# Dilated mixer of a hybrid decoder layer: a written order with weight halves split two steps ahead, softmax sums transposed before they go to DRAM, and first scores at the end of the gate projection

## The chip, the core and the metric

The kernel runs on one core of one Trainium2 chip. The metric is the device time of one execution in microseconds (us). Before the change the runs have a median of 2697.38 us over three runs (2695.77 to 2700.28). The engines are named as in the profile: PE multiplies (PEld are its weight loads), ACT is the scalar engine, DVE the vector engine, POOL the gpsimd engine, and SP only issues DMAs. DMAs are also issued by ACT and POOL, each in the order of its own instructions.

## What is computed

One decoder layer over 512 tokens of width 2048, in float32: a modulated RMSNorm gives `u`; one wide projection of `u` feeds three token mixers (differential attention, retention, dilated windows); each mixer's output is multiplied by a SiLU gate, projected, weighted by a sigmoid gate and summed; an output projection, a residual and a last norm follow. The change touches the dilated mixer only:

```
for each of 8 heads, three groups (window, dilation) = (128,1), (512,4), (2048,16), head dim 128:
    s_g   = q_g @ k_g^T / sqrt(128), masked to t, t-d, ..., t-window
    o_g   = softmax(s_g) @ v_g ;  den_g = log sum exp(s_g)
    o     = sum_g softmax over g (den_g) * o_g
y_C = o * silu(z_C)            # z_C: gate columns of the projection of u
```

With 512 tokens the second and third group are both sets of tokens that are equal modulo 4 (the third additionally masked), so both are computed on the same strided view, and their exponentials and sums are taken over one row of 2 x 128 scores against a common lowest score. The first group (a band of 128 tokens) is computed apart, with its own lowest score and its own sum; the two are merged by weights for which the first group's lowest scores and sums are needed in the strided token order.

## The kernel before

**Arithmetic.** Every float32 operand is split into a high part (ACT copies it to the multiply type) and a low part (DVE subtracts that copy from the original). A product is three matmuls, high x high, high x low and low x high (`mm3`, L164 to L166).

**Stages.** Before the mixer a long stage of block products writes most projections of `u` to DRAM: the queries of all groups, the keys of the first and second (`qk_dram`) and the values (`v_dram`). Only the third group's keys and the gate `z` are projected in the mixer itself. The mixer stands between 1372.71 and 1671.23 us of the profiled execution; the gate phase of its output projection follows.

**The mixer before (L844 to L1048).** A loop over 8 heads; each head does:

- The projection of the third group's keys: two weight halves of 1024 x 128 (512 KB), each loaded by SP (L136, tile `wr`), split by ACT (L159, `wh`) and DVE (L160, `wl`), then multiplied (24 matmuls of 128x512). Between the halves, the head before is turned (`turn`: 8 transposes of its exponentials, L931, split by L205/L206 into `p1`, `p2`), and the second group's scores are taken (`scores(1)`, L897/L899).
- After both halves: the values' products of the head before (`values`, L944/L946, and `mm3` for the first group), `first_turn` (7 transposes, L882, split by L885/L886 into `p0`), and the split of the projected keys out of PSUM (`split_pairs`, tile `kc<-pj`, L205/L206).
- The values of the head are loaded (L1000) and split (L1002/L1003), and the first group's query and key of the next head are loaded straight into `ql` and `kc` (`first_inputs`, L977/L978) and split (L979 and L982 on ACT, L980 and L983 on DVE). `qh`, `ql` and `kc` have two buffers each.
- The projection of `z`, again two halves. Between them: the third group's scores (`scores(2)`, L897/L899 with the projected keys), the masked negated scores with row minima on DVE (L903, L839), the exponentials on ACT (L913), the merge weights (`wt`), and then the first scores and first exponentials of the next head (`first_scores`: `mm3`, L839, L865).
- SiLU (sigmoid on ACT L211, product on DVE L213), and the next head's second query and key (`turned`, L988, L197/L198, L205/L206).

Two round trips through DRAM turn columns into rows. The first group's row minima and sums (`st1`, 128 partitions x 2 x 4 values) are written by a DMA that ACT issues (L869, `bounce<-st`, element by element with a stride of 512 bytes in partition order) and read back by a DMA that POOL issues (L870, `st<-bounce`) in strided token order. The merge weights `wt` are written likewise (L922) and read back broadcast to all partitions (L924, `wtb<-bounce`), where POOL multiplies them into the SiLU gate (`weigh`, L962) and DVE into the first group's output (L957).

**What sets the order.** The stage before the mixer is pinned: `pin` marks its matmuls, splits and loads to stay in the order of the program. The mixer is not: there, the scheduler of the tile layer puts each engine's instructions in an order of its own choice, and each engine then works through its list strictly in that order, waiting at an instruction whose inputs or buffers are not ready.

Of the kernel before, what the change touches and what calls it, by code (L numbers as in the profile page):

```python
# [2 lines left out]

# [61 lines left out]
def hybrid_kernel(ctx, tc, x, c, w_in, w_pa, w_pb, w_pc, w_out, w_ada, b_ada, norm_w, lam,  # L65
# [3 lines left out]
    act = nc.scalar  # L69
    dve = nc.vector  # L70
# [34 lines left out]
    nc.sync.dma_start(out=ident, in_=k_ident)  # L105
# [28 lines left out]
    def w_load(src, k0, c0):  # L134
        r, h, l = w_tiles([P, 8, P])
        nc.sync.dma_start(out=r, in_=src[k0:k0 + 1024, c0:c0 + P].rearrange("(j p) c -> p j c", p=P))  # L136
        return r, h, l

    pinned = [False]

    def pin(instr):

        if pinned[0]:
            tc.keep_in_program_order(instr)

    def w_half(src, k0, c0, rot=False, tiles=None, low=dve):
# [11 lines left out]
        else:  # L158
            pin(act.copy(h, r))  # L159
            pin(low.tensor_sub(l, r, h.bitcast(F32)))  # L160
        return h, l

    def mm3(ps, ah, al, bh, bl, start, stop):
        pin(nc.tensor.matmul(ps, lhsT=ah, rhs=bh, start=start, stop=False))  # L164
        pin(nc.tensor.matmul(ps, lhsT=ah, rhs=bl, start=False, stop=False))  # L165
        pin(nc.tensor.matmul(ps, lhsT=al, rhs=bh, start=False, stop=stop))  # L166
# [16 lines left out]
    def split(pool, tag, ps, shape=None, scale=None, view=None, bufs=1):  # L183

        shape = shape or [P, S]
        h = pool.tile(shape, F32R, tag=tag + "h", name=tag + "h", bufs=bufs)
        l = pool.tile(shape, F32R, tag=tag + "l", name=tag + "l", bufs=bufs)
# [14 lines left out]
    def split_pairs(pool, tag, src, bufs=1):  # L202

        t = pool.tile([P, 4, 2, P], F32R, tag=tag, name=tag, bufs=bufs)
        act.copy(t[:, :, 0, :], src)  # L205
        dve.tensor_sub(t[:, :, 1, :], src, t[:, :, 0, :].bitcast(F32))  # L206
        return t
# [8 lines left out]
    def v_load(pool, unit, c0, tag, strided=False):  # L216
# [4 lines left out]
        nc.sync.dma_start(out=r, in_=src.rearrange("(i r) c -> i r c", r=4) if strided  # L221
# [17 lines left out]
    nc.sync.dma_start(out=smalls[0:16, :], in_=c.rearrange("o (j p) -> (o j) p", p=P))  # L239
    nc.sync.dma_start(out=smalls[16:32, :], in_=norm_w.rearrange("o (j p) -> (o j) p", p=P))  # L240
    nc.sync.dma_start(out=smalls[32:80, :], in_=b_ada.rearrange("o (j p) -> (o j) p", p=P))
    nc.sync.dma_start(out=smalls[80:81, :], in_=da_w)
    nc.sync.dma_start(out=smalls[81:82, :], in_=ret_w)
    xt = [xq.tile([P, D], F32, tag=f"x{i}", name=f"x{i}") for i in range(NT)]
    for i in range(2):
        nc.sync.dma_start(out=xt[i], in_=x[0, i * P:(i + 1) * P, :])
# [8 lines left out]
    def mod_load():  # L255
# [10 lines left out]
        nc.sync.dma_start(out=wa, in_=w_ada[0, part * nk * P:(part + 1) * nk * P, half * D + c0:half * D + c0 + cw]  # L266
# [7 lines left out]
    def load_first(i):  # L274
# [3 lines left out]
        nc.sync.dma_start(out=r, in_=w_in[k * P:(k + 1) * P, g0:g0 + NF * P].rearrange("p (b c) -> p b c", c=P))  # L278
# [9 lines left out]
    nc.sync.dma_start(out=xt[2], in_=x[0, 2 * P:3 * P, :])  # L288
    for q in range(2):
        nc.sync.dma_start(out=xt[3][:, q * 1024:(q + 1) * 1024], in_=x[0, 3 * P:4 * P, q * 1024:(q + 1) * 1024])  # L290
# [10 lines left out]
    nc.tensor.transpose(tp[:, 0:P], smalls, ident)  # L301
# [25 lines left out]
    def mod_cols(m):  # L327
# [5 lines left out]
        for ci in range(nch):  # L333
            for a in range(chains):
                nc.tensor.matmul(pc[:, ci:ci + 1], lhsT=acc[:, a, ci * P:(ci + 1) * P], rhs=ones[:, 0:1],
# [31 lines left out]
    def x_tr(tp, i, k):  # L367
        nc.tensor.transpose(tp[:, i * P:(i + 1) * P], xt[i][:, k * P:(k + 1) * P], ident)
# [54 lines left out]
    for i, (phase, k) in enumerate(steps):  # L423
# [21 lines left out]
        for b in range(NF):  # L445
            nc.tensor.matmul(ps[b], lhsT=h[:, b, :], rhs=uh[k], start=k == 0, stop=False)
        if i + 1 < 2 * KC and i + 1 != KC and (i + 1) in group_of:
            mod_cols(group_of[i + 1])
        for b in range(NF):
            nc.tensor.matmul(ps[b], lhsT=h[:, b, :], rhs=ul[k], start=False, stop=False)  # L450
        for b in range(NF):
            nc.tensor.matmul(ps[b], lhsT=l[:, b, :], rhs=uh[k], start=False, stop=k == KC - 1)
# [28 lines left out]
    nc.sync.dma_start(out=lamt, in_=lam.rearrange("o a b -> (o a b)").partition_broadcast(P))  # L481
# [924 lines left out]
```

## Time and profile before

| | |
|---|---|
| runs, median (lowest to highest) | 2697.38 us (2695.77 to 2700.28) |
| the profiled execution's own time | 2697.8 us |
| its span, first to last instruction | 2696.0 us |
| PE busy, share of the span | 2563.4 us, 95% |
| DVE busy | 1912.5 us, 71% |
| ACT busy | 1130.1 us, 42% |
| mixer, 1372.71 to 1671.23 | 298.52 us: PE 259.64, DVE 180.41, ACT 159.30, POOL 21.62 busy |
| mean granted TensorE clock, whole span / mixer | 0.979 / 0.92 |

How to read the profile: times are microseconds from the span's start. A group of instructions is one line of the kernel, one engine and one operation, `out<-in` by tile names. In brackets stands the time that the engine stood idle just before an instruction, and the instruction or DMA that ended that wait. PE's busy time includes matmuls that run at a lower granted clock.

### The profile page before, as it was taken

Reading aid. Unit: us, or ns where it says so; the run is one execution under the profiler, and the core shown is the slowest. Engines: PE = TensorE matmul, PEld = TensorE weight load, DVE = VectorE, ACT = ScalarE, POOL = GpSimd, SP = SyncE. Lnnn points to the kernel's source line nnn. Section 1 sums busy time; section 2 is a strip of 40 time slices with the busy share of each in tenths; the row PEclk is TensorE's granted clock in tenths of the full one; section 3 lists DMA queues with packets and bytes.
Section 4 is the critical chain, followed back from the end, with each engine's and each line's share of the span. In section 5 each row is a group of like instructions: output and inputs, shape, how many; then the busy total and the mean of one; then the engine's idle time right before and its main releaser. Section 6 shows DMA issues by size and latency. Waiting matters only on the chain.

```text
span 2696.0 us, 36917 instructions
## 1 busy us (share of the span) xinstructions
PE 2563.4 (95%) x14531; PEld 2246.5 (83%) x14531; DVE 1912.5 (71%) x2646; ACT 1130.1 (42%) x1453; POOL 293.5 (11%) x336
## 2 busy tenths in 40 slices
PE   6999999999999999999998898999999989999898
PEld 5777778999999999998877777888888778878678
DVE  7995878777788777888766565357677457676674
ACT  4233433433334333333345555246666235553222
POOL 2331002221122212121000000000000000000000
PEclk9999999999999999999998999999999989999999
DMA  9776666666666666666665555552323563336862
GB/s 346 246 277 234 220 206 232 233 223 207 208 218 229 225 222 221 200 225 227 229 169 129 122 116 135 178 153 81 95 84 88 171 198 99 101 97 199 298 224 103
DMA packets 394418, 503.33 MB, mean 187 GB/s; under 512 B 27170, under 2 KB 258420, under 8 KB 393092
## 3 DMA queue, kind: packets, MB, share of 16 engines
q1 hardware_dynamic: 364484, 448.89, 52.9%
q0 software_dynamic: 10048, 35.23, 4.1%
q10 hardware_dynamic: 19712, 16.85, 1.8%
q8 instruction: 114, 1.87, 0.3%
q14 instruction: 60, 0.49, 0.1%
HBM read 449.39 MB, written 51.51 MB: 186 GB/s over the span
## 4 chain that ended last, share of the span: by engine, by line
PE 67%; DVE 13%; DMA 13%; ACT 4%; issue 3%; SPq 0%; ACTq 0%; DVEq 0%
PE at L166 11%; PE at L165 11%; PE at L164 11%; PE pj L164 10%; PE pj L165 10%; PE pj L166 10%; DVE acc L324 4%; DMA gpr<-part 2%; DMA ql<-qk 2%; DVE xl L513 2%; DMA gwa<-in_w_ada_dram 2%; DMA xr<-in_w_in_dram 1%; DMA gsg<-g 1%; DVE xr L598 1%; DVE wl L160 1%
## 5 line engine op out<-in xcount | busy, mean ns | idle before, releaser
L512 ACT CAST xh<-xr 128x2048 fp32r<-128x2048 f32 x196 | 374.3, 1910 | 586.9 <-PE at L165 349.1
L513 DVE TENSOR_TENSOR xl<-xr,xh 128x2048 fp32r<-128x2048 f32 x196 | 452.0, 2306 | 194.1 <-ACT xh L512 192.5
L166 PE MATMUL pj<-uh,wl 128*128 128x512 f32 x912 | 360.1, 395 | 5.7 <-DVE wl L157 3.1
L164 PE MATMUL pj<-uh,wh 128*128 128x512 f32 x912 | 363.6, 399 | 0.8 <-ACT wh L156 0.8
L165 PE MATMUL pj<-ul,wh 128*128 128x512 f32 x912 | 359.5, 394 | 0.0
L598 DVE TENSOR_TENSOR xr<-xr 128x512 f32<-128x512 f32 x448 | 329.8, 736 | 18.5 <-DMA xr<-in_w_in_dram 7.0
L160 DVE TENSOR_TENSOR wl<-wr,wh 128x1024 fp32r<-128x1024 f32 x146 | 178.1, 1225 | 121.1 <-ACT wh L159 116.7
L166 PE MATMUL at<-fh,xl 128*128 128x256 f32 x864 | 246.0, 285 | 4.3 <-DVE xl L513 4.3
L164 PE MATMUL at<-fh,xh 128*128 128x256 f32 x864 | 245.2, 284 | 0.0
L165 PE MATMUL at<-fl,xh 128*128 128x256 f32 x864 | 245.2, 284 | 0.0
L159 ACT CAST wh<-wr 128x1024 fp32r<-128x1024 f32 x148 | 154.5, 1050 | 204.3 <-PE pj L165 84.4
L166 PEld LDWEIGHTS pj<-uh,wl 128*128 128x128 f32 x912 | 173.6, 190 | 43.0 <-DVE wl L157 3.5
L164 PEld LDWEIGHTS pj<-uh,wh 128*128 128x128 f32 x912 | 174.6, 191 | 35.5 <-ACT wh L156 1.3
L165 PEld LDWEIGHTS pj<-ul,wh 128*128 128x128 f32 x912 | 174.1, 191 | 34.5
L166 PEld LDWEIGHTS at<-fh,xl 128*128 128x128 f32 x864 | 166.2, 192 | 5.6 <-DVE xl L513 5.5
L165 PEld LDWEIGHTS at<-fl,xh 128*128 128x128 f32 x864 | 166.3, 192 | 0.0
L164 PEld LDWEIGHTS at<-fh,xh 128*128 128x128 f32 x864 | 166.2, 192 | 0.0
L165 PE MATMUL at<-ul,xh 128*128 128x256 f32 x576 | 163.0, 283 | 0.0
L164 PE MATMUL at<-uh,xh 128*128 128x256 f32 x576 | 163.0, 283 | 0.0
L166 PE MATMUL at<-uh,xl 128*128 128x256 f32 x576 | 163.0, 283 | 0.0
L164 PE MATMUL at<-yh,wh 128*128 128x512 f32 x336 | 132.7, 395 | 6.4 <-DVE gsg L809 6.4
L165 PE MATMUL at<-yl,wh 128*128 128x512 f32 x336 | 131.8, 392 | 0.0
(421 smaller groups left out, 5954.0 us busy)
## 6 DMA issues: line engine op xcount, KB each, us to landing
xr<-in_w_in_dram SPq DMA_DIRECT2D x224, 512.0 KB, 4.5
xr<-in_w_in_dram SPq DMA_DIRECT2D x84, 1024.0 KB, 5.1
wr<-in_w_in_dram SPq DMA_DIRECT2D x116, 512.0 KB, 3.9
wa<-in_w_ada_dram SPq DMA_DIRECT2D x20, 1024.0 KB, 9.7
wr<-in_w_out_dram SPq DMA_DIRECT2D x32, 512.0 KB, 4.7
gwa<-in_w_ada_dram SPq DMA_DIRECT2D x32, 512.0 KB, 4.9
wr<-in_w_in_dram SPq DMA_DIRECT2D x32, 448.0 KB, 7.1
wb<-in_w_ada_dram SPq DMA_DIRECT2D x12, 1024.0 KB, 10.6
```

What stands on the lines that cost most here:

```text
L159: pin(act.copy(h, r))
L160: pin(low.tensor_sub(l, r, h.bitcast(F32)))
L164: pin(nc.tensor.matmul(ps, lhsT=ah, rhs=bh, start=start, stop=False))
L165: pin(nc.tensor.matmul(ps, lhsT=ah, rhs=bl, start=False, stop=False))
L166: pin(nc.tensor.matmul(ps, lhsT=al, rhs=bh, start=False, stop=stop))
L324: dve.scalar_tensor_tensor(out=acc, in0=wa[:, j, :], scalar=sc[:, k:k + 1], in1=acc, op0=ALU.mult, op1=ALU.add)
L512: pin(act.copy(h, r))
L513: pin(dve.tensor_sub(l, r, h.bitcast(F32)))
L598: pin(dve.tensor_add(r[:, o, :], r[:, o, :], r[:, a, :]))
```

## The change

- **Pinning.** All instructions of ACT, DVE, PE and SP now go through a wrapper that marks them to keep program order while `pinned[0]` is set. Where the stage before the mixer pinned its instructions one by one, the wrapper does the same. `pinned[0]` is now also set for the whole mixer. (In the changed kernel, instructions issued through the wrapper carry its line, L86.)
- **A written pipeline.** The mixer's 32 weight halves are steps: of head `hd`, steps `4 * hd` and `4 * hd + 1` are the two halves of the third keys' projection (k0, k1 from here on), `4 * hd + 2` and `4 * hd + 3` those of the gate `z` (z0, z1). `half_step(n)` issues in this order: the load of half n+4, extra loads of the mixer, the split of half n+2, the work that was put off until here (`late`), and the 24 matmuls of half n. Scores, turns and values stand between the steps.
- **First scores** of the next head move from the middle of the z projection to its end.
- **First sums.** `st1` is turned on PE (one transpose to 8 x 128), copied by ACT to a row tile and written by one DMA with 8 rows of 512 bytes. It is issued after the second half of the k projection, and POOL reads it back as before.
- **Small things.** The raw third and second queries and the second keys have a tile each (`r2`, `r3`, `r4`) instead of two shared buffers `rq`; `lows` has one buffer instead of two; the mask `tri` is a part of the `band` tile, and its DMA is dropped; values, first queries and keys are loaded and split in separate functions so that each can be placed.

The core of the diff:

```diff
+    class Ordered:
+        def __init__(self, engine):
+            self.engine = engine
+        def __getattr__(self, name):
+            f = getattr(self.engine, name)
+            return lambda *a, **k: pin(f(*a, **k))
+
+    act, dve, pe, sync = (Ordered(e) for e in (nc.scalar, nc.vector, nc.tensor, nc.sync))
...
-            bounce = dram.tile([2, S], F32, tag="bounce", name="bounce", bufs=2)
-            nc.scalar.dma_start(out=bounce.rearrange("s (a p) -> p s a", p=P), in_=st1)
-            nc.gpsimd.dma_start(out=st[:, 2:4, :], in_=bounce.rearrange("s (i r) -> i s r", r=4))
+        def first_sums():
+            tp = at()
+            pe.transpose(tp[0:8, 0:P], ctx_["st1"].rearrange("p s a -> p (s a)"), ident)
+            row = cp.tile([8, P], F32, tag="row", name="row")
+            act.copy(row, tp[0:8, 0:P])
+            bounce = dram.tile([8, P], F32, tag="bounce", name="bounce", bufs=2)
+            act.dma_start(out=bounce, in_=row)
+            nc.gpsimd.dma_start(out=ctx_["st"][:, 2:4, :], in_=bounce.rearrange("(s a) (i r) -> (a i) s r", s=2, r=4))
...
+    def half_step(n, *extra):
+        half_load(n + 4)
+        for f in extra:
+            f()
+        if loads:
+            entry.append(w_half(w_in, 0, 0, tiles=loads.pop(0)))
+        due, late[:] = list(late), []
+        for f in due:
+            f()
+        half_mul(n)
...
+    for hd in range(8):
+        h, prev = heads[hd], heads[hd - 1] if hd else None
+        def more():
+            got["raw3"] = load_turned(4, hd)
+            if hd < 7:
+                got["raw2"] = load_turned(2, hd + 1), load_turned(3, hd + 1)
+        half_step(4 * hd, more)
+        if prev:
+            prev.turn()
+            prev.weigh(sz)
+        else:
+            h.first_scores(*first[0], first[1])
+            late.append(h.first_exps)
+        h.scores(1, *second[0], second[1])
+        def more():
+            third[:] = query_tiles(), key_tiles()
+            if hd < 7:
+                got["first"] = load_first_qk(hd + 1)
+        late.append(lambda: split_query(got["raw3"], third[0]))
+        half_step(4 * hd + 1, more)
+        split_keys(half_ps[0], third[1])
+        if prev:
+            h.first_sums()
+            prev.values(vs)
+            h.first_turn()
+            late.append(lambda: prev.finish(sz))
+        if hd < 7:
+            late.append(lambda: split_first_qk(*got["first"]))
+        half_step(4 * hd + 2, lambda: got.update(vs=load_values(hd)))
...
+        h.scores(2, *third[0], third[1])
+        late.append(h.exps)
+        if hd < 7:
+            late.append(lambda: got.update(
+                second=(split_query(got["raw2"][0], query_tiles()), split_keys(got["raw2"][1], key_tiles()))))
+        half_step(4 * hd + 3)
+        sz = silu(cp, half_ps[0], bufs=1)
+        vs = got["vs"]
+        if hd < 7:
+            heads[hd + 1].first_scores(*got["first"][0], got["first"][1])
+            late.append(heads[hd + 1].first_exps)
+            second = got["second"]
+        late.append(lambda vs=vs: split_values(vs))
```

How instructions move is shown at three places. The first is ACT in a middle head, around the split of the projected third keys (`kc<-pj`); the numbers are those of tile buffers. Before:

```order
L205 CAST p1_13052<-at_13047 128x4x128
L205 CAST p2_13060<-at_13055 128x4x128
L979 ACTIVATE qh_13193<-ql_13194 128x512
L159 CAST wh_13342<-wr_13341 128x1024
L205 CAST kc_13175<-pj_13016 128x4x128
L950 COPY gpr_13113<-at_13114 128x2x128
L950 COPY gpr_13113<-at_13125 128x2x128
L982 CAST kc_13195<-kc_13195 128x4x128
L885 CAST p0h_13154<-at_13156 128x512
```

And with the change:

```order
L86 CAST p1_13081<-at_13076 128x4x128
L86 CAST p2_13089<-at_13084 128x4x128
L86 CAST wh_12952<-wr_12951 128x1024
L86 ACTIVATE qh_13116<-r4_13033 128x512
L86 CAST kc_13118<-pj_13051 128x4x128
L86 COPY row_13156<-at_13154 8x128
L86 DMA bounce_13158<-row_13156 8x128
L86 COPY gpr_13161<-at_13162 128x2x128
L86 COPY gpr_13161<-at_13173 128x2x128
L86 CAST p0h_13199<-at_13201 128x512
L86 CAST p0h_13199<-at_13208 128x384
L86 CAST wh_13030<-wr_13029 128x1024
```

The next head's first query (`qh<-ql`, with `ql` filled by a DMA) stood two rows ahead of the split of the projected keys; now a weight half and the third query (`qh<-r4`) stand there, and `qh<-ql` follows behind the last row shown, after one copy of the mixer's output (`yh`). The copy of the sums' row and its DMA are new.

The second place is PE between the two halves of a z projection (`at<-kc,qh` are scores, `pj<-` a projection). Before:

```order
L166 MATMUL pj_12878<-uh7_111,wl_12881 128x512
L897 MATMUL at_12909<-kc_12851,qh_12847 128x256
...
L899 MATMUL at_12918<-kc_12851,ql_12848 128x128
L164 MATMUL at_12946<-kc_12871,qh_12869 128x128
...
L166 MATMUL at_12955<-kc_12871,ql_12870 128x256
L164 MATMUL pj_12878<-uh8_112,wh_12972 128x512
```

And with the change, where the last five rows are those from the end of the z projection on:

```order
L86 MATMUL at_12933<-kc_12790,qh_12788 128x256
...
L86 MATMUL at_12942<-kc_12790,ql_12789 128x128
L86 MATMUL pj_12908<-uh8_112,wh_12624 128x512
...
L86 MATMUL pj_12908<-uh15_119,wl_12625 128x512
L86 MATMUL at_13011<-kc_12793,qh_12791 128x128 x2
L86 MATMUL at_13011<-kc_12793,ql_12792 128x128
...
L86 MATMUL at_13020<-kc_12793,ql_12792 128x256
L86 MATMUL pj_13051<-uh0_104,wh_12702 128x512
```

The first scores (8 tiles of `at` with high and low keys of the next head) stood directly behind the third scores; now the second half of z lies between them, and the next k projection follows them.

The third place is DVE from the third scores to the SiLU product. Before, with the rows that read a row minimum left out:

```order
L903 TENSOR_TENSOR lows_14219<-at_14214,tri4_12388 128x256
L839 ISA e1_14239,st1_14241<-at_14242,band_12384 128x128
...
L910 TENSOR_REDUCE low_14223<-st_13916 128x4
L839 ISA e1_14239,st1_14241<-at_14251,band_12384 128x256
...
L213 TENSOR_TENSOR sz_14299<-pj_14174,gsg_14297 128x512
```

And with the change:

```order
L86 TENSOR_TENSOR lows_14259<-at_14254,tri4_12390 128x256
...
L86 TENSOR_TENSOR wl_14098<-wr_14096,wh_14097 128x1024
L86 TENSOR_REDUCE low_14269<-st_13993 128x4
...
L86 SCALAR_TENSOR_TENSOR ql_14286<-r2_14019,qh_14285 128x512
L86 TENSOR_TENSOR kc_14289<-r3_14021,kc_14289 128x4x128
L86 TENSOR_TENSOR sz_14318<-pj_14220,gsg_14316 128x512
L86 ISA e1_14320,st1_14322<-at_14323,band_12388 128x128
```

`low<-st`, which reads the sums' tile that came back from DRAM, stood among the next head's first scores (`e1`); now it stands directly behind a weight half's low part, and the first scores follow the SiLU product.

332 lines of the change are left out of this document (171 added, 161 removed).

## The prediction, on record before the changed kernel was run

> **What bounds the kernel now.** PE is busy for 95% of the span, so I looked for what lengthens PE's own time, stage by stage. The first view is the table of busy time by stretch, cut at the mixer and at two of its heads (duration, then PE, PEld, DVE, ACT, POOL busy, granted clock, DMA share, GB/s):
>
> ```profile
> 1372.71:1671.23 298.52, 259.64 (x1302) 220.33 (x1301) 180.41 (x440) 159.30 (x303) 21.62 (x25) 0.92 0.57 132
> 1489.50:1526.75 37.25, 32.97 (x169) 28.55 (x167) 23.01 (x57) 20.11 (x40) 2.60 (x3) 0.91 0.56 123
> 1567.62:1602.84 35.22, 31.77 (x169) 27.53 (x168) 22.69 (x56) 19.04 (x37) 2.60 (x3) 0.95 0.57 122
> ```
>
> In the mixer PE stands idle for 298.52 - 259.64 = 38.9 us and has 0.92 of its clock. These heads take 35 and 37 us, in which DVE works 23 and ACT 19 to 20, so neither is full. The second view, the waits of the mixer (total, times, longest), names what PE waits for:
>
> ```profile
> ACT qh L979 <- DMA ql<-qk: 77.3, 7, 14.8
> POOL st L870 <- DMA bounce<-st: 59.5, 5, 30.1
> PE at L897 <- DVE kc L206: 29.2, 7, 7.5
> ```
>
> Three quarters of PE's idle time is one wait, seven times: the third scores (L897) wait for the low part of the projected keys. The timeline of one head shows why (start, duration, idle before):
>
> ```profile
> 1500.16 1.32 SPq L977 DMA_DIRECT2D ql<-qk  x1
> 1506.57 0.63 ACT L979 ACTIVATE qh<-ql 128x512 fp32r<-128x512 f32 x1 [12.00 <-DMA ql<-qk]
> 1508.04 0.58 ACT L205 CAST kc<-pj 128x512 fp32r<-128x512 f32 x1
> 1509.83 0.69 DVE L206 TENSOR_TENSOR kc<-pj,kc 128x512 fp32r<-128x512 f32 x1
> 1510.67 0.55 PE L897 MATMUL at<-kc,qh 128*128 128x256 f32 x1 [4.28 <-DVE kc L206]
> ```
>
> The projection of those keys was done at 1500. Their copy (L205) stands behind the next head's first query (L979), which waits 12.00 us for a load that SP issues only at 1500.16. So an instruction that nobody needs yet blocks ACT, then DVE, then PE. The clock makes it dearer:
>
> ```profile
> 1437.61 0.33 PE L164 MATMUL at<-kc,qh 128*128 128x128 f32 x1 [2.05 <-ACT kc L982]
> 1438.20:1441.60 3.40, 3.27 (x13) 3.17 (x14) 3.37 (x7) 2.36 (x6) 0.00 (x0) 0.50 0.30 79
> 1611.19 0.39 PE L944 MATMUL at<-p,vh 128*128 128x256 f32 x1 [0.90 <-DVE p L206]
> 1612.00:1616.00 4.00, 4.00 (x35) 3.95 (x35) 1.24 (x10) 0.00 (x0) 0.00 (x0) 1.00 0.67 42
> ```
>
> A wait of 2.05 us is followed by 3.40 us at half clock (1.7 lost), one of 0.90 us is not. The Trainium skill, "TensorE: Matmul & The Clock Gate", section "Why this matters for your kernels", allows idle gaps up to about 3 us before the clock falls to half; the row of 2.05 us is against that limit, so I go by the row, and by the page the waits of 1.5 to 2 us that rival A below speaks of would cost no clock and A would end some 4 us lower.
>
> **PE's own work.** A stretch without waits at full clock gives the price of each block:
>
> ```profile
> 1489.50 1.04 PE L931 MATMUL at<-ident,e 128*128 128x128 f32 x8
> 1490.30 0.36 PE L897 MATMUL at<-kc,qh 128*128 128x256 f32 x1
> 1491.25 0.46 PE L164 MATMUL pj<-uh,wh 128*128 128x512 f32 x1
> 1496.80 0.28 PE L944 MATMUL at<-p,vh 128*128 128x256 f32 x1
> 1499.96 0.95 PE L882 MATMUL at<-ident,e 128*128 128x128 f32 x7
> 1500.67 0.48 PE L164 MATMUL pj<-uh,wh 128*128 128x512 f32 x1
> 1404.60 0.33 PE L164 MATMUL at<-kc,qh 128*128 128x128 f32 x1 [0.55 <-ACT qh L979]
> 1406.37 0.39 PE L165 MATMUL pj<-ul,wh 128*128 128x512 f32 x1
> ```
>
> From start to start: turn 0.80, scores 0.95, a weight half 5.55, values 3.16, first turn 0.71, first scores 1.77. A head is four halves (22.20), two scores (1.90) and the rest (6.44): 30.54. Eight heads less the turn and values of the last, which fall to the gate phase (3.96), are 240.4. The added transposes (one 8x128 for each head; eight of 128x128 take 0.80) cost 0.1 each: 241.1 in all. That fits the stage: 298.5 less 38.9 idle less 0.08 x 298.5 = 23.9 of clock is 235.7, which is too low by the idle time inside half-clock windows, counted twice. So the most that any order can gain here is 298.5 - 241.1 = 57.4 us.
>
> **The change, part by part.** *The queue.* In the written order `qh<-ql` goes behind `kc<-pj`, the values and the first turn, and its load is asked for after `scores(1)`, a head's part earlier. From there to its split PE has a half, the values, the first turn (9.4 us); the load takes 6.3:
>
> ```profile
> ql<-qk SPq DMA_DIRECT2D x8, 256.0 KB, 6.3
> bounce<-st ACTq DMA_DIRECT2D x8, 4.0 KB, 11.4
> st<-bounce POOLq DMA_DIRECT2D x8, 4.0 KB, 5.6
> bounce<-wt ACTq DMA_DIRECT2D x7, 4.0 KB, 3.9
> wtb<-bounce POOLq DMA_DIRECT2D x7, 512.0 KB, 9.2
> ```
>
> (KB each, median us from issue to landing.) The keys' split is ready 0.58 + 0.69 = 1.3 us after k1; the third scores come 3.16 + 0.71 + 5.55 = 9.4 us after it. The wait of 29.2 us goes. *First scores at the end of z* need their query 5.55 us later than before, which adds to that margin and costs nothing. What is queued behind them is the next exponentials on ACT, and for those the k0 half is cover.
>
> *What is late next.* From the start of z1 ACT must do, before it can split the turned scores: exponentials, second query and key, sigmoid, two weight halves, first exponentials, three values, two turn splits. Its rows and DVE's (count, total, mean ns):
>
> ```profile
> L159 ACT CAST wh<-wr 128x1024 fp32r<-128x1024 f32 x23 | 23.4, 1045 | 10.6 <-DMA wr<-in_w_proj_c_dram 10.6
> L913 ACT ACTIVATE e<-e,low 128x256 f32<-128x256 f32 x24 | 11.9, 495 | 0.0
> L197 ACT ACTIVATE qh<-rq 128x512 fp32r<-128x512 f32 x11 | 12.4, 1125 | 0.0
> L211 ACT ACT_TABLE_LOAD x6 | 7.7, 1283 | 0.7 <-ACT e L865 0.6
> L160 DVE TENSOR_TENSOR wl<-wr,wh 128x1024 fp32r<-128x1024 f32 x23 | 27.6, 1223 | 9.6 <-ACT wh L159 9.6
> L903 DVE TENSOR_TENSOR lows<-at,tri 128x256 f32<-128x256 f32 x22 | 8.7, 421 | 0.0
> L839 DVE CUSTOM_DVE_ANT_0 e<-at,lows 128x128 f32<-128x128 f32 x44 | 10.5, 290 | 0.0
> ```
>
> With these, less about 0.1 for each overlap with the next, and 0.5 to 0.6 for the 128x512 copies, ACT's list is about 14.8 us and DVE's last split makes it 15.5; PE needs from z1 to the values 5.55 + 1.77 + 5.55 + 0.80 + 0.95 + 5.55 = 20.2. Of the 4.7 us between, about 4 are gone: the exponentials start late by DVE's masked scores (two of L903, four of L839, with overlap 1.6), weight half (1.2) and `low`, and the handoffs take some tenths. I take a wait of 0.3 us for each steady head (bounds 0 and 1.5): 6 x 0.3 = 1.8. In head 1 the two queues first fill (its second query and key are split behind those of head 0): walking the rows through the order gives 2.3 and 2.2 us in front of its scores and values, 4.5, with one half-clock window, 1.7 (bounds 0 and 10).
>
> *The start.* The first query cannot be split earlier than DVE is through with the stage before:
>
> ```profile
> 1376.56 1.28 DVE L633 TENSOR_TENSOR z<-at,z 128x512 f32<-128x512 f32 x2
> 1383.56 0.38 SPq L977 DMA_DIRECT2D ql<-qk  x1
> 1372.71 0.39 PE L164 MATMUL pj<-uh,wh 128*128 128x512 f32 x1
> ```
>
> Its load now stands ahead of the weight loads that held it until 1383.56. DVE is free at 1377.84; two splits of 0.7 make 1379.2, when PE has been through k0 for 0.95 us; the second splits add some 0.5: 1.5 (bounds 0 and 8, since head 0 might wait for its load as before).
>
> *Sums transposed.* After k1: keys' copy 0.6, row copy 0.3, issue 0.4, a write like that of `bounce<-wt` 3.9, the read 5.6: 10.8 us. `low` stands on DVE 3.16 + 0.71 + 5.55 + 0.95 + 1.6 + 1.2 = 13.2 us after k1. Margin 2.4, cost nothing; without it each us late is one us in ACT's list. The new write has eight rows, the old one 1024 elements; its price lies between 3.9 and 11.4, and I take 3.9, because the `wt` write is as scattered and still takes that. *Merge weights:* issued some 6 us into z1 and needed behind the values, 20.2 + 3.2 us after its start: 3.9 + 9.2 = 13.1 against 17; POOL's read of the sums stands behind `weigh`. *Weight halves two ahead:* 29.2 of PE's 38.9 us are the keys', and the full-clock stretch above runs through two halves without a wait on weights, so no gain of its own. *The dropped mask load, tile names, `lows`:* nothing; SP had issued them beside PE's work.
>
> Sum: 241.1 + 1.5 + 4.5 + 1.7 + 1.8 = 250.6 against 298.5, a gain of 47.9. The profiled execution's own time is 2697.8 (span 2696.0, 1.8 around it): 2649.9; its time stands 0.4 above the median of the runs, so 2649.5, rounded to **2649 us**.
>
> **Rivals.** *A: ACT and DVE set the pace.* If their lists are 5% longer than my sum, the margin is used up and each of seven heads waits 1.5 us more, with a third of a half-clock window on average (0.5): + 14, 2663 us. For it: only tenths are left of the 4.7 us. Against: in the heads above ACT was busy 20 of 30.5 us. By the Trainium skill, "ScalarE: Activation LUTs", section "What ACT_TABLE_LOAD costs", a switch of tables costs 2.66 us with its drain, not the load's 1.28; two switches in each head would then add 2.8 us to ACT's list and give about 2665. The rows
>
> ```profile
> 1482.80 1.28 ACT L865 ACT_TABLE_LOAD   x1
> 1484.09 0.40 ACT L865 ACTIVATE e<-e,st 128x128 f32<-128x128 f32 x1
> ```
>
> show the next activation 0.01 us behind the load, so no drain after it; the trace does not agree and I give that form a small part of A's chance.
>
> *B: the sums' round trip is late.* If the new write takes 11.4 like the old one, the chain is 18.3, 5.1 us over the 13.2, and 7 heads lose 36: 2685. For it: POOL's waits above show this round trip as slow and queued. *Slower:* the same mechanism with its read held up too, since POOL's read stands behind `weigh` and that behind the broadcast: 11.4 + 9.2 = 20.6 for write and read. Beyond about 12 us of round trip each us costs one in each head (some 7.5 of them, the first and last being short); the gain of 47.9 is gone at 12 + 47.9 / 7.5 = 18.4, and 20.6 gives + 65: 2714. *C: the wait only moves,* or PE finds another one of 4 us to 6 us in each head (values' loads, L1002): about 2697. Against: the query's load, 6.3 us, is the longest that ACT is left to wait for, and has 9.4 us of cover.
>
> **How the numbers follow.** Forecast 0.53 (own range 2636 to 2656), better than that 0.07, since head 1 and the start may cost nothing (2638 down to 2632), A 0.21, B 0.08, C 0.04, slower 0.07. The range from 2632 to 2676 holds the forecast, A with a window in every head, and the gains. A difference of 0.2%, 5.4 us, is about what this measurement tells from none. Faster 0.53 + 0.07 + 0.21 + 0.08 = 0.89, same 0.04, slower 0.07.
>
> **What would show it.** Right: a mixer of about 250 us with clock 0.98 or more, no wait of L897 on the keys' split, `ql` waits gone from ACT, PE waits only before the scores and values of head 1, `bounce` written within 4 us. A: waits of 1 to 3 us at the values (L944) on `p` or `vl` in every head. B: `low` waits on `st`, ACT idle before L913. Wrong altogether: a mixer above 290.

## The result

The changed kernel takes 2651.72 us (median of four runs, 2647.57 to 2654.36) against 2696.57 us before (median of four runs in the same rounds): a ratio of 0.983, with a 95% interval from 0.9813 to 0.9848, that is 45 us less. In later rounds beside the experiments it came out at 0.9844 (0.983 to 0.9859). The prediction was 2649 us, with a range from 2632 to 2676. One execution of a later version, the profiled one of the attempt at the start, took 8837.93 us at a granted clock of 0.43 and counts in no time given here.

The mixer in the table of busy time by stretch (duration, then PE, PEld, DVE, ACT, POOL busy, granted clock, DMA share, GB/s), from its first matmul to the first one of the gate phase:

```profile
1373.21:1625.92 252.71, 243.10 (x1309) 207.70 (x1308) 187.05 (x438) 161.74 (x309) 21.96 (x25) 0.99 0.53 156
```

It took 298.52 us before, so the stage gives 45.8 us; the rest of the span went from 2397.5 to 2399.1 us. Idle time of PE in the stage fell from 38.9 to 9.6 us, and the granted clock rose from 0.92 to 0.99. The waits of PE that remain are these (total, times, longest):

```profile
PE at L86 <- ACT kc L86: 4.4, 1, 4.4
PE at L86 <- DVE p L86: 4.0, 8, 1.1
PE at L86 <- DVE kc L86: 0.8, 2, 0.4
```

The wait of 29.2 us for the low part of the third keys is gone. In its place stands one wait of 4.4 us at the very start, and in three heads about 1 us ahead of the values, for the turned scores `p`:

```profile
1383.22 0.33 PE L86 MATMUL at<-kc,qh 128*128 128x128 f32 x1 [4.41 <-ACT kc L86]
1546.91 0.39 PE L86 MATMUL at<-p,vh 128*128 128x256 f32 x1 [1.14 <-DVE p L86]
```

The DMAs changed more than the prediction had expected. First the packets, MB and share of ACT's DMA queue, then KB and median us to landing of each kind in the mixer:

```profile
q10 hardware_dynamic: 2032, 0.06, 0.5%
...
wr<-in_w_in_dram SPq DMA_DIRECT2D x29, 512.0 KB, 3.9
vl<-vd SPq DMA_DIRECT2D x24, 256.0 KB, 4.9
wtb<-bounce POOLq DMA_DIRECT2D x7, 512.0 KB, 5.1
ql<-qk SPq DMA_DIRECT2D x8, 256.0 KB, 4.2
st<-bounce POOLq DMA_DIRECT2D x8, 4.0 KB, 3.2
bounce<-wt ACTq DMA_DIRECT2D x7, 4.0 KB, 1.7
```

Before, the queue had 10224 packets in the mixer, 8192 more, as many as eight heads of 1024 single elements. And transfers other than the sums' own are faster than before: `wr` 3.9 us where it was 5.2, `wtb` 5.1 (9.2), `ql` 4.2 (6.3). Not all are: the raw queries and keys (`r`, before `rq`) take 4.1 us where they took 3.3. The packets:

```profile
q10 hardware_dynamic: 10224, 0.06, 1.8%
```

are the row of the kernel before. So besides the order, something else changed: the transfers that the order waits for. The experiments take the two apart as far as they can.

### The profile page after: what moved, and what is told of

It is laid out like the page before. It is cut to its first block, busy times and chain, and to the rows that moved or that the text cites. A ratio compares the mean times of both kernels' runs of the same rounds, so it can differ in the third digit from the quotient of the medians.

```text
span 2651.8 us, 36979 instructions
## 1 busy us (share of the span) xinstructions
PE 2543.9 (96%) x14539; PEld 2231.4 (84%) x14539; DVE 1919.4 (72%) x2646; ACT 1132.2 (43%) x1461; POOL 290.5 (11%) x336
## 5 line engine op out<-in xcount | busy, mean ns | idle before, releaser
L86 ACT CAST xh<-xr 128x2048 fp32r<-128x2048 f32 x196 | 374.2, 1909 | 584.7 <-PE at L86 494.3
L86 DVE TENSOR_TENSOR xl<-xr,xh 128x2048 fp32r<-128x2048 f32 x196 | 451.2, 2302 | 195.5 <-ACT xh L86 193.9
L86 ACT CAST wh<-wr 128x1024 fp32r<-128x1024 f32 (+2 forms) x275 | 240.2, 890 | 324.0 <-PE at L86 102.4
L86 PE MATMUL pj<-uh,wl 128*128 128x512 f32 x944 | 370.8, 393 | 5.9 <-DVE wl L86 3.3
L86 PE MATMUL pj<-uh,wh 128*128 128x512 f32 x944 | 373.6, 396 | 2.9 <-ACT wh L86 2.3
L86 PE MATMUL pj<-ul,wh 128*128 128x512 f32 x944 | 369.6, 392 | 0.0
L86 DVE TENSOR_TENSOR wl<-wr,wh 128x1024 fp32r<-128x1024 f32 (+2 forms) x241 | 240.9, 1013 | 142.2 <-ACT wh L86 141.3
L86 DVE TENSOR_TENSOR xr<-xr 128x512 f32<-128x512 f32 x448 | 329.1, 735 | 18.0 <-DMA xr<-in_w_in_dram 6.7
L86 PE MATMUL at<-fh,xl 128*128 128x256 f32 x864 | 246.2, 285 | 4.5 <-DVE xl L86 4.4
L86 PE MATMUL at<-fl,xh 128*128 128x256 f32 x864 | 245.3, 284 | 0.0
L86 PE MATMUL at<-fh,xh 128*128 128x256 f32 x864 | 245.2, 284 | 0.0
L86 PEld LDWEIGHTS pj<-uh,wl 128*128 128x128 f32 x944 | 178.1, 189 | 44.7 <-DVE wl L86 4.5
L86 PEld LDWEIGHTS pj<-uh,wh 128*128 128x128 f32 x944 | 178.6, 189 | 38.1 <-ACT wh L86 2.7
L86 PEld LDWEIGHTS pj<-ul,wh 128*128 128x128 f32 x944 | 178.6, 189 | 35.1
L86 PEld LDWEIGHTS at<-fh,xl 128*128 128x128 f32 x864 | 166.6, 193 | 5.9 <-DVE xl L86 5.5
L86 PEld LDWEIGHTS at<-fh,xh 128*128 128x128 f32 x864 | 166.6, 193 | 0.0
L86 PEld LDWEIGHTS at<-fl,xh 128*128 128x128 f32 x864 | 166.6, 193 | 0.0
L86 PE MATMUL at<-uh,xl 128*128 128x256 f32 x576 | 163.1, 283 | 0.0
L86 PE MATMUL at<-ul,xh 128*128 128x256 f32 x576 | 163.1, 283 | 0.0
L86 PE MATMUL at<-uh,xh 128*128 128x256 f32 x576 | 163.1, 283 | 0.0
L86 PE MATMUL at<-yh,wh 128*128 128x512 f32 x336 | 132.0, 393 | 6.4 <-DVE gsg L86 6.4
L86 PE MATMUL at<-yh,wl 128*128 128x512 f32 x336 | 131.4, 391 | 0.0
```

The source lines that it names most:

```text
L86: return lambda *a, **k: pin(f(*a, **k))
```

## The experiments

Each ratio below is to the kernel before, in the same rounds. The changed kernel is at 0.983 in the first rounds and 0.9844 in the last.

### The order alone, in the kernel before

The first run takes the kernel before and fixes only the place of the next head's first query in the lists of ACT and DVE: the copies and subtractions of `split_pairs`, of the query in `first_inputs` and of `head_values` go through `pin`, which acts between the two lines that set it.

```diff
-        third = turned(4, hd), split_pairs(cp, "kc", perm(ps), bufs=2)
-        vs = head_values(hd)
+        third = [turned(4, hd)]
+        pinned[0] = True
+        third.append(split_pairs(cp, "kc", perm(ps), bufs=2))
+        pinned[0] = False
+        pinned[0] = True
         if hd < 7:
             first = first_inputs(hd + 1)
+        vs = head_values(hd)
+        pinned[0] = False
```

> The kernel before, its order still chosen by the scheduler, with one thing fixed: ACT and DVE split the projected third keys (kc<-pj) ahead of the next head's first query (qh<-ql), and that query ahead of the values. Theory (a blocked in-order queue): PE's wait of 29.2 us for kc<-pj at L897 goes to below 5. But qh<-ql still waits for its load, and the first scores, still in the middle of z, need it some 0.95 us later, so a wait of 2 to 3 us at the first scores takes its place; with less half-clock time: 2675 us, 2662 to 2687. Rival (the gain needs the weight pipeline): within 5 us of 2697. Rival (no wait moves): 2655 or less.

Measured: 2685.44 us, 0.9966 (0.9949 to 0.9984). The waits of PE:

```profile
PE at L897 <- DVE gpr L951: 8.9, 5, 2.6
PE at L897 <- DVE kc L206: 4.1, 4, 1.8
PE at L165 <- DVE kc L983: 4.0, 4, 3.4
```

The wait for the keys' split fell from 29.2 to 4.1 us, as the theory said, and another one took its place, but not only where it was expected. ACT still stands at the query (49.3 us in seven waits), now with the copies of the values' output behind it; DVE's `gpr` sums come late, and the third scores wait for them (for the PSUM tiles that `gpr` reads, as far as the names tell). Taking one instruction out of the way of a blocked queue passes the wait to the next one in line. The gain is at the small end of the range.

The second run also moves the first scores to the end of z.

```diff
         def closing():
             scores(2, *third[0], third[1])
-            if hd < 7:
-                head[0](*first[0], first[1])
         sz = silu(cp, proj(C_Z + hd * P, mid=closing), bufs=1)
+        if hd < 7:
+            head[0](*first[0], first[1])
```

> As the run with the keys split first, and the next head's first scores moved from the middle of z to its end, as in the change; weights, sums and the rest stay as before. Theory: with these two moves the waits at both kinds of scores are gone, and nearly the whole gain of the change is there without the weight pipeline and without transposed sums: 2658 us, 2648 to 2670. Rival (the weight pipeline or the sums carry a good part): above 2675.

Measured: 2702.66 us, 1.0033 (1.0019 to 1.0047), slower than before. The theory falls here: the two moves do not carry the gain.

```profile
PE at L931 <- ACT e L913: 11.1, 18, 3.1
PE at L944 <- DVE p L206: 9.2, 7, 2.0
PE at L897 <- DVE gpr L951: 6.6, 4, 2.5
```

ACT waits even longer than in the first run for the load of `ql` (57.5 us in seven waits), and what is behind it, the exponentials and the turned scores, is late now. In both runs that load takes over 10 us to land (10.8 and 10.4), where the changed kernel's takes 4.2. In these two runs the order only chose who pays for a late load.

### Pinning

```diff
-    pinned[0] = True
     half_load(3)
     heads = [c_head(hd) for hd in range(8)]
```

> The changed kernel with its mixer not pinned: same program, but the scheduler orders ACT, DVE, PE and SP. Its list puts qh<-ql three rows ahead of kc<-pj on ACT again, while the first scores stay at the end of z and PE's order is that of the change. Theory: the query's load is asked for after scores(1) and lands about 5 us later, near the end of the second key half, so ACT is blocked for little, and the third scores have 9.4 us of cover: 2660 us, 2648 to 2675. Rival (pinning itself is the gain): 2685 to 2700. The wait of ACT at qh<-ql and of PE at the third scores tell them apart.

Measured: 2643.96 us, 0.981 (0.9793 to 0.9828), faster than the range expected. Pinning itself is no part of the gain; the scheduler's order of the same program is at least as good. ACT now waits for `ql` once, 3.9 us, although the query stands ahead of the keys' split again, and PE's waits are

```profile
PE at L86 <- ACT e L86: 2.3, 5, 1.3
PE at L86 <- DVE p L86: 1.2, 6, 0.3
PE at L86 <- ACT kc L86: 0.8, 1, 0.8
```

The start costs less here: three weight halves run ahead of head 0's first scores (16.5 us), where the pinned order has one. In the trace the mixer takes 247.8 us, 4.9 less than when pinned. Against the changed kernel the difference is 0.2 to 0.34%. It was measured in other rounds and is at the limit of what the intervals tell apart: this run's reaches up to 0.9828, those of the changed kernel begin at 0.9813 and 0.983.

### The sums' write

The old write in the changed kernel, at the new place:

```diff
-            tp = at()
-            pe.transpose(tp[0:8, 0:P], ctx_["st1"].rearrange("p s a -> p (s a)"), ident)
-            row = cp.tile([8, P], F32, tag="row", name="row")
-            act.copy(row, tp[0:8, 0:P])
-            bounce = dram.tile([8, P], F32, tag="bounce", name="bounce", bufs=2)
-            act.dma_start(out=bounce, in_=row)
+            bounce = dram.tile([2, S], F32, tag="bounce", name="bounce", bufs=2)
+            act.dma_start(out=bounce.rearrange("s (a p) -> p s a", p=P), in_=ctx_["st1"])
```

> The changed kernel with the first group's sums written as before, by one DMA of 1024 single elements straight from st1, at the same place in the order; no transpose, no row copy. Rival B of the prediction: the write takes about 11 us, the chain 18.3 against 13.2, low waits for st, ACT is blocked before the exponentials: 2685 us (2672 to 2695). Other theory (the round trip has more cover than I gave it, since the margin of 2.4 us is not all): 2652 to 2660.

Measured: 2676.73 us, 0.993 (0.9907 to 0.9953): some 23 to 27 us of the 45 are lost (against 0.9844 and 0.983).

```profile
ACT e L86 <- DVE low L86: 37.1, 7, 9.9
DVE low L86 <- DMA st<-bounce: 14.7, 5, 6.7
...
wr<-in_w_in_dram SPq DMA_DIRECT2D x29, 512.0 KB, 6.4
vl<-vd SPq DMA_DIRECT2D x24, 256.0 KB, 11.6
bounce<-st ACTq DMA_DIRECT2D x8, 4.0 KB, 10.3
st<-bounce POOLq DMA_DIRECT2D x8, 4.0 KB, 6.1
```

Rival B's mechanism is real: `low` waits for the sums in five heads, up to 6.7 us, where the changed kernel has no such wait, and ACT's exponentials wait 37.1 us for `low`, where they wait 24.8 there. But `vl`, a load that has nothing to do with the sums, also went from 4.9 to 11.6 us.

The same part of the change alone, in the kernel before, at its old place behind the first exponentials:

```diff
-            nc.scalar.dma_start(out=bounce.rearrange("s (a p) -> p s a", p=P), in_=st1)
-            nc.gpsimd.dma_start(out=st[:, 2:4, :], in_=bounce.rearrange("s (i r) -> i s r", r=4))
+            nc.tensor.transpose(tp[0:8, 0:P], st1.rearrange("p s a -> p (s a)"), ident)
...
+            act.copy(row, tp[0:8, 0:P])
...
+            nc.scalar.dma_start(out=bounce, in_=row)
+            nc.gpsimd.dma_start(out=st[:, 2:4, :], in_=bounce.rearrange("(s a) (i r) -> (a i) s r", s=2, r=4))
```

> The kernel before with one part of the change alone: the first group's sums turned on PE (8x128), copied by ACT and written as 8 rows of 512 bytes, at their old place (behind the first exponentials, mid z); order still the scheduler's. Contention theory (from the runs so far: with the element write, the load of ql took 10.4 to 10.8 us, without it 3.0 to 4.2): the load of the next head's first query lands in 3 to 5 us instead of 6.3, the weight loads ahead of it too, so ACT is blocked less at qh<-ql and PE's wait for the split keys falls by half or more: 2675 us (2662 to 2688). Rival (the write is harmless where it stood): 2690 to 2700.

Measured: 2661.23 us, 0.9897 (0.9879 to 0.9914). This one part, without any new order, has about 30 us of the 45, just past the good end of the range that the contention theory gave.

```profile
1371.31:1633.50 262.19, 245.53 (x1310) 208.91 (x1309) 185.74 (x452) 163.32 (x316) 21.63 (x25) 0.97 0.54 151
...
PE at L869 <- ACT e L865: 10.7, 6, 2.5
PE at L165 <- DVE kc L987: 4.0, 1, 4.0
PE at L164 <- ACT kc L986: 1.7, 1, 1.7
...
ACT qh L983 <- DMA ql<-qk: 33.4, 7, 7.0
```

The wait for the third keys is gone altogether, although the query is still ahead of them in ACT's list: ACT's wait for `ql` fell from 77.3 to 33.4 us, and what is left of it ends before PE needs the keys. The weight loads land in 4.9 us and the broadcast `wtb` in 4.1 instead of 9.2. Why the query's load was late in the kernel before stands in SP's and ACT's rows there:

```profile
1458.01 7.05 SPq L977 DMA_DIRECT2D ql<-qk  x1
1488.81 0.37 ACTq L869 DMA_DIRECT2D bounce<-st  x1
1494.00 6.07 SPq L136 DMA_DIRECT2D wr<-in_w_in_dram  x2
```

In one head SP stood for 7.05 us in the issue of the query's load itself, while a write of the sums issued at 1450.68 was under way. In the next, the write of the sums was issued at 1488.81 and landed by 1500.36, when POOL issued its read; SP stood for 6.07 us in the issues of two weight loads, until 1500.07, and so issued the query's load only at 1500.16, the row that the prediction shows. With the row write the longest of these issues of `ql` takes 1.17 us. The rival here is the round trip's own length: in the kernel before, `low` waits for the sums once, 6.0 us in the first head, with a wait of PE of 5.0 us behind it, and that is gone too. It can be the smaller part of the 30 us only; the wait for the keys was 29.2. A new small wait shows what the written order does better: the transposes (L869) stand in the middle of z, right behind the exponentials that they need, and wait for them in six heads.

The old write again in the changed kernel, but issued right behind the first exponentials:

```diff
                                bias=st1[:, 0, i:i + 1], accum_out=st1[:, 1, i:i + 1])
+            sums_out()
...
         def first_sums():
...
+            pass
+
+        def sums_out():
...
```

> The changed kernel with the element write of the sums, issued right behind the first exponentials (in k0) and not after k1, some 8 us earlier. If the run with the old write lost its 25 us by the round trip's length alone, that length has cover again here: 2650 to 2658 us. If it lost them because the 1024 single elements hold up the other loads meanwhile: 2662 to 2680, with loads of vl, r or wr at 7 us or more.

Measured: 2659.14 us, 0.988 (0.9865 to 0.9895). No wait of `low` for the sums is left, and loads are slow all the same:

```profile
vl<-vd SPq DMA_DIRECT2D x24, 256.0 KB, 8.8
ql<-qk SPq DMA_DIRECT2D x8, 256.0 KB, 6.2
bounce<-st ACTq DMA_DIRECT2D x8, 4.0 KB, 11.3
```

The time lies between the two ranges. Against 0.993 at the new place, the early write gets back 0.005, some 13 us, which were the late sums; some 10 to 13 us of the 23 to 27 remain when the sums are in time. The intervals leave about 7 us either way, so both theories are right in part, and the split is rough.

Last, a write that nobody reads:

```diff
             act.dma_start(out=bounce, in_=row)
...
+            scratch = dram.tile([2, S], F32, tag="scratch", name="scratch", bufs=2)
+            act.dma_start(out=scratch.rearrange("s (a p) -> p s a", p=P), in_=ctx_["st1"])
```

> The changed kernel with one DMA more in each head, directly behind the new row write: the old element write of the sums (1024 single elements) to a place that nothing reads. No instruction waits for it but the next user of its source two heads later. Contention theory: the elements hold up the other loads as in the run with the old write (vl there 11.6 us, in the changed kernel 4.9): vl at 8 us or more, 2658 to 2672 us. Latency theory (only the wait for the sums cost time there): vl at 5 us, 2648 to 2656 us.

Measured: 2673.88 us, 0.9934 (0.992 to 0.9949), 24 us above the changed kernel in the same rounds and just past the range of the contention theory. Three rows of its loads, then the table by stretch for the 10.4 us behind one of these writes:

```profile
wr<-in_w_in_dram SPq DMA_DIRECT2D x29, 512.0 KB, 9.0
vl<-vd SPq DMA_DIRECT2D x24, 256.0 KB, 12.4
st<-bounce POOLq DMA_DIRECT2D x8, 4.0 KB, 11.6
...
1461.10:1471.50 10.40, 10.40 (x57) 9.38 (x58) 9.68 (x16) 5.39 (x9) 0.76 (x1) 0.89 0.22 22
```

And the changed kernel, in the same 10.4 us of the same head:

```profile
1454.40:1464.80 10.40, 10.40 (x62) 9.18 (x62) 9.68 (x18) 4.95 (x10) 0.76 (x1) 1.00 0.62 162
```

In both stretches SP wants to load weights and values. With 1024 single elements under way the core moves 22 GB/s, without them 162. It is more than a late landing: SP itself is held, as the durations of its three issues of `vl` in that step of the head before show (ns, shortest, median, longest), with the idle write

```profile
L86 SPq DMA_DIRECT2D vl<-vd x3: 529/1353/6379, 1430.4 to 1432.4; - x3
```

and without it

```profile
L86 SPq DMA_DIRECT2D vl<-vd x3: 530/622/1128, 1425.6 to 1427.4; - x3
```

This shows the contention. It does not split the 24 us as cleanly as it was meant to: the sums' own read (`st<-bounce`) is among the loads held up, 11.6 us where it was 3.2, so that `low` waits for it too (11.5 us in four heads).

### Depth, place of the first scores, and ACT's list

Weight halves loaded three and split one ahead:

```diff
-        half_load(n + 4)
+        half_load(n + 3)
...
-        if loads:
+        if loads and n:
...
-    half_load(3)
```

> The changed kernel with weight halves loaded three and split one step ahead instead of four and two. Theory (splits are never late here, PE waited for none): 2648 to 2658 us, as the changed kernel. Rival (the depth matters): PE waits for wl in each head, 2665 or more.

Measured: 2649.47 us, 0.9843 (0.9828 to 0.9858), equal to the changed kernel. PE does wait for a low part now, 0.5 to 2.0 us in six heads, 5.4 us in all, but the waits for `p` are gone: the time is spent inside a weight half, and no longer before the values.

First scores back in the middle of z:

```diff
+        if hd < 7:
+            heads[hd + 1].first_scores(*got["first"][0], got["first"][1])
+            late.append(heads[hd + 1].first_exps)
         half_step(4 * hd + 3)
         sz = silu(cp, half_ps[0], bufs=1)
...
-            heads[hd + 1].first_scores(*got["first"][0], got["first"][1])
-            late.append(heads[hd + 1].first_exps)
```

> The changed kernel with the next head's first scores back in the middle of z, behind the third scores. Theory: the query's load was asked for after scores(1) and has landed, but its split stands behind the output copy yh, which waits for POOL's weigh; the first scores wait 0 to 1.5 us in each head: 2655 us (2648 to 2666). Rival (the move to the end of z carries the gain): 2670 or more, with a wait of 3 us or more at the first scores.

Measured: 2655.69 us, 0.9869 (0.9851 to 0.9887), as the theory had it: five waits for the first keys, 1.2 us each but for the start.

```profile
PE at L86 <- ACT kc L86: 8.7, 5, 3.8
PE at L86 <- DVE kc L86: 3.7, 7, 0.6
```

By the ratios the move to the end of z is worth 7 to 10 us of the gain, but the intervals overlap.

Two more copies in ACT's list:

```diff
         if loads:
-            entry.append(w_half(w_in, 0, 0, tiles=loads.pop(0)))
+            tiles = loads.pop(0)
+            if n and n % 4 == 0:
+                for _ in range(2):
+                    act.copy(tiles[1], tiles[0])
+            entry.append(w_half(w_in, 0, 0, tiles=tiles))
```

> The changed kernel with two more copies of a weight half (2.1 us) in ACT's list in the k0 step of heads 1 to 7, between the sigmoid and the turn's splits. Rival A of the prediction says that ACT's list sets the pace: each head waits some 2 us more at the values, 14 to 16 us in all, and with waits then of 2 to 3 us half-clock windows come on top: 2666 to 2680 us. If there are still 2 us of slack in the list: 2650 to 2657.

Measured: 2666.04 us, 0.9896 (0.9875 to 0.9917), 15.8 us above the changed kernel in the same rounds (14 by the ratios) for 7 x 2.1 = 14.7 us of work. The kernel grows by about as much as was added, but not by waiting alone. PE's waits for `p` grow only from 4.0 to

```profile
PE at L86 <- DVE p L86: 10.7, 12, 2.3
```

and the rest is clock: the mixer's granted clock is 0.95, where it was 0.99. Here the price is one for one, then, by waits and half clock together; how much slack the list still had before the clock fell, this run does not separate. One of these waits, and the stretch behind it:

```profile
1422.07 0.38 PE L86 MATMUL at<-p,vh 128*128 128x256 f32 x1 [1.28 <-DVE p L86]
1423.40:1426.80 3.40, 3.40 (x18) 3.40 (x18) 3.26 (x10) 1.96 (x5) 0.76 (x1) 0.50 0.03 7
```

### An attempt at the start

```diff
         else:
+            half_step(1)
             h.first_scores(*first[0], first[1])
-            late.append(h.first_exps)
         h.scores(1, *second[0], second[1])
...
```

(with the third query's and keys' splits of head 0 behind it)

> A version meant to be faster: the changed kernel, and only in head 0 the first and second scores stand behind k1 instead of k0, so that the first queries' and keys' loads and splits have 5.55 us more. Theory: the waits of 4.41, 0.40 and 0.44 us at the start and the half clock behind them go: 7 us less than the changed kernel in the same rounds (4 to 9). Rival (the wait moves to the third keys or the sums of head 0): within 2 us of it.

Measured: 2648.44 us (median of four executions), 0.9839 (0.9825 to 0.9852), against 2650.22 us and 0.9844 for the changed kernel beside it:

> The changed kernel itself, in the same rounds, as the measure for the other three: 0.983 of the kernel before, as measured (0.981 to 0.985).

The difference of 1.8 us is within the intervals. The theory of 7 us is not borne out; the rival's "within 2 us" is what came, but its reason (the wait moves on) is not shown. Where the time went instead is open: the one trace of this version cannot be set beside the others.

## Why the prediction was right, and which terms were not

**The bound.** PE's waits in the mixer and the clock behind them were what could be gained, and a ceiling of 57 us from PE's own work holds: 252.7 less 9.6 idle, less 3.0 for the one stretch of 6.80 us at half clock (whose idle time is left out), is 240.1, where the prediction had 241.1.

```profile
1383.70:1390.50 6.80, 6.11 (x23) 5.53 (x24) 5.70 (x18) 6.38 (x11) 0.00 (x0) 0.50 0.87 290
```

**The cause.** The time was forecast well, but by a mechanism that is only half of what happened. The step that was too narrow is the reading of the blocked query. That ACT's in-order list holds the keys behind a late load is right, but the prediction took the lateness as given and let the order cure it. The runs show where the lateness came from: with the sums in rows alone the wait is gone in the old order, and with the order of the query alone it only moves. Nor is it the query's new place in ACT's list that cures it: left to the scheduler, the changed kernel has the query ahead of the keys again, and its time is at least as good (0.981). The prediction said of the transposed sums "cost nothing" and looked at their own round trip; as a part by itself it is worth about 30 us. The rows that could have told it were there before: SP's 7.05 us in one issue of `ql` and 6.07 us in two of `wr`, and 10224 packets for 0.06 MB in ACT's queue. That the number came out all the same is in part luck: the row write was in the change, for another reason, and without it the new order is at 0.993. The Trainium skill, "DMA: Bandwidth & Descriptors", section "Rules for kernel authors", says that a last dimension that is not contiguous becomes one descriptor for each element and should be rearranged. The 8192 packets less agree with it; that such a DMA also holds up others is not in that rule, and the runs show it.

**How the parts add up.** The new order with the old write is at 0.993, or 0.988 with the write issued early; the row write in the old order is at 0.9897; both together at 0.983. Each alone gets some 40 to 70% of the gain. The likely reason is that both remove the same waits: the row write lets the load land early, the order asks for it sooner and needs it later.

**The sum's terms.** The start was put at 1.5 us and took 5.25 (4.41 + 0.40 + 0.44), and 3.0 of clock. The step that failed is "its load now stands ahead of the weight loads that held it": so it does, but it stands behind the load of `band` in SP's list, and that one, as far as the times tell, waits for the memory of the stage before:

```profile
1361.40 2.09 SPq L86 DMA_DIRECT2D wr<-in_w_in_dram  x3
1373.40 0.34 SPq L86 DMA_DIRECT2D band<-in_k_band_dram  x1
...
1374.80 0.52 SPq L86 DMA_DIRECT2D ql<-qk  x1
1380.74 0.63 ACT L86 ACTIVATE qh<-ql 128x512 fp32r<-128x512 f32 x1 [12.56 <-DMA ql<-qk]
```

SP stands still until 1373.40, when PE's last matmul of that stage is done (the profile names an instruction of DVE, but that one had long ended). DVE's part of the query's split starts 3.07 us after DVE is free, and the first key, loaded behind the query, is what PE waits for last: ACT copies it only at 1382.55. Head 1 was put at 4.5 + 1.7 us and took 0.15; that the delay at the start gave ACT and DVE their lead is likely, but no run shows it. The steady heads were put at 1.8 us in all and took 3.9, within the bounds. These errors of 6.8 and 2.1 one way and 6.0 the other nearly cancel, so the total is better than its terms, and that too is luck. The sums' chain has more room than was reckoned: its write landed in about 1.8 us and its read in 3.2, where 3.9 and 5.6 were put. The ground for the 3.9, that the `wt` write "is as scattered" as the old one of the sums, was misread: the idle write adds 8320 packets for eight writes, 1040 each, and of the kernel before this leaves 1904 for seven of `wt`, 272 each. Of the signs that it named, the mixer's length and clock came and the wait for the third keys went; but ACT still waits once for `ql` (12.56 us), and PE's waits stand at the start and in three later heads, not in head 1.

**The rivals.** A did not happen, but it is close at hand: 14.7 us more in ACT's list made the kernel 15.8 us longer, though more by the clock and less by waits than A had it. Its form with dearer table switches, 2.8 us more in each head, would have had to show in the waits at the values: with 2.1 us more they reach 2.3 us, and in the changed kernel the longest is 1.14. B did not happen, and the old write shows why it was a danger: its 36 us came out as 23 to 27. The slower rival did not happen either, and no run has its round trip of 20.6 us: with the idle write the sums' read took 11.6 us, but their own write went out in rows, and a gain was still left. C, the wait that only moves, came in the kernel before with the query moved (0.9966), and with the first scores moved too nothing was gained (1.0033). Two ahead was worth nothing over one ahead, as predicted; pinning, which the prediction did not price, was worth nothing either.

## What to carry to other kernels

When an in-order list is held by a late load, look for what makes the load late before changing who stands behind it: moved alone, the wait went to the next instruction. A tiny DMA written element by element can cost the loads that run beside it far more than itself; if the tile can be turned first, let it leave in rows. And when a queue's first load of a stage is late, read what stands ahead of it, down to the smallest constant.

## What the runs showed of the hardware

- In the run with the idle write, one DMA of 1024 elements of 4 bytes kept the core's transfers down to 16 to 22 GB/s for 10 us in three heads, where the same stretches of the changed kernel had 138 to 163, and SP stood in the issue of one load for 6.4 us. In the kernel before, whose loads stand elsewhere, three such stretches had 36 to 106 GB/s. The row of ACT's queue there counts only 1.8% of the engines' time for its packets, so that share does not show it. Which part of the DMA path such a write fills is not shown.
- The granted clock fell to half for 3.4 us behind a wait of PE of 1.28 us; behind waits of up to 1.14 us in the changed kernel it did not. The length of the wait alone does not decide it: with the first scores in the middle of z, three waits of 1.21 to 1.24 us were followed by half clock and a fourth of 1.21 us was not, and with the row write in the old order one of 2.28 us was not. What else decides is not shown. The Trainium skill, "TensorE: Matmul & The Clock Gate", section "Why this matters for your kernels", puts the bound at gaps of about 3 us; these runs do not agree.
